# One net on one core: first norm, low-rank parts, scan products and log_dt loads rewritten

## The chip, the cores and the metric

The kernel runs on one core of a Trainium2 chip, as one program. The metric is the device time of a launch in microseconds, here the median of several runs. TensorE (PE in the profile) does the matrix products, VectorE (DVE) and ScalarE (ACT) the elementwise work, GpSimd (POOL) small powers and some memory moves, SyncE (SP) issues most of the transfers. All values are fp32. Each fp32 product appears as two PE instructions in the profile. The large weights are split into a high and a low part of 12 significant bits each, and a product then takes three instructions of a single pass ("mm3").

## The reference

The input is one sequence of 1024 tokens of 1024 features (D). Two layers and a hybrid block follow.

- Layer 0: RMS norm, a gated linear recurrence mixer ("hawk", width 1280), then a SwiGLU feed-forward part (width 2816) and a per-layer embedding: `h = h + (p[0] @ wp) * sigmoid(rms_norm(h) @ wg)`.
- Layer 1: RMS norm, an RWKV-7 time mix with 16 heads of 64, then the same feed-forward part and embedding with their own weights.
- A last RMS norm, then a block with a convolution of 31 taps and a complex diagonal state space of 32 groups with 64 states (S5), whose step sizes are `dt = exp(log_dt)`, one for each group.

The time mix is what most of the change touches. It shifts the tokens by one and makes six mixes of each token with the one before it; three go into r, k and v, three into low-rank parts:

```python
w = -softplus(-(w0 + tanh(xw @ w1) @ w2)) - 0.5      # w1: D x 64, w2: 64 x D
a = sigmoid(a0 + (xa @ a1) @ a2)                     # a1: D x 64, a2: 64 x D
g = sigmoid(xg @ g1) @ g2                            # g1: D x 160, g2: 160 x D
S_t = S_{t-1} * decay_t + (S_{t-1} a_t) b_t^T + v_t k_t^T      # for each head, 64 x 64
y_t = S_t r_t
out = (group_norm(y) + sum(r * k * r_k) * v) * g @ w_o
```

Here a_t is minus the normalized key of a head and b_t that key times `a`.

## The kernel before

Activations lie feature-major: 128 features on the partitions, tokens along the free axis, in two halves of 512 tokens. The first two layers run one after the other: hawk until about 500 us, the first feed-forward part until 1190, the embedding, then the time mix from about 1340 to 2395 ("scan stage"), the second feed-forward part to 3170, the second embedding, and the hybrid block to the end. The S5 parameters are prepared by `s5_prep`, whose steps are issued between those of the scan's end and of the second feed-forward part.

**First norm.** `load_rows` brings in 512 tokens as four tiles of 128 tokens x 1024 features; `turn_rows` transposes them on PE into feature-major tiles `h`. `square` then squares each of the eight tiles on ACT (L312) and adds them up on DVE (L313). `rstd_bcast` sums over the partitions on PE (L273), takes the power on GpSimd (L290), and spreads the factor over all partitions on PE (L281). L328 scales the tiles.

**Scan stage.** Its parts are Python generators that yield a step (engine, estimated us, what it waits for, a PSUM bank to take or give back) before the instructions of that step. `weave_` keeps a rough clock for each engine and always issues the step that would start first. So the order on every queue is written by estimates, and a changed estimate moves steps everywhere in the stage. PSUM banks by tag: two `mm`, three `g`, two `ch`, one `y`.

- `rwkv_dense` takes four segments of 256 tokens. A segment has 28 units: 24 of 128 columns for r, k and v (mm3, L249 to L251), and four for the first low-rank factors (L885, plain fp32). The two that belong to `w` and `a` (mixes 1 and 4) use the same 128 weight columns, 64 of `w1` beside 64 of `a1`; each computes all 128 and keeps half. Then `finish` runs for each of the eight head pairs of a segment. `lora2` multiplies the second low-rank factors (L926): 64 rows for w, 64 for a, 128 and 32 for g. Keys are normalized: per-head sums on PE (`heads_sum`, L1431), the reciprocal on DVE, and `heads_bcast` (L1438), which gives every feature of a head its token's value. Results go to DRAM.
- `rwkv_scan` takes 16 chunks of 64 tokens. `inner` (L1100) multiplies keys and queries in a chunk: for four head pairs at a time, first the four even heads (partitions 0 to 63) into one `g` bank, then the four odd heads (64 to 127) into another; DVE masks each bank (L1104). `diagonal`, `blocks`, `inverse`, `inverted` and `whole` invert a triangular matrix: its 32 x 32 blocks by substitution on DVE and GpSimd, with a way through DRAM (stores L1157, loads L1168, both on SP's queue), the rest by products L1179 and L1189. `chain` carries the state S (L1244 to L1274). `outs` makes y from the state (L1289, 64 x 64) and from the chunk itself (L1291, 128 x 64), and `post` does the group norm and the gate, again with `heads_bcast`.
- `rwkv_out` is the last projection.

**log_dt.** `s5_prep` first loads the S5 parameters on GpSimd's queue. The 32 values of log_dt go to all partitions (L1479). Then two further loads (L1481) bring the even groups' values to the lower and the odd ones' to the upper 64 partitions, every second value of the row.

Of the kernel before, what the change touches and what calls it, by code (L numbers as in the profile page):

```python
# [14 lines left out]
P = 128  # L15
# [41 lines left out]
class Net:  # L57
    """Feature-major activations: tile [128 features, 512 tokens] per (k, half)."""
# [16 lines left out]
    def open_group(self, T, W, S, L, psum):  # L75
        """Pools of one part of the net: T and S slots of [128, 516], weight slots, PSUM banks per tag."""
# [6 lines left out]
    def open_work(self, W, S, L, psum):  # L83
        """All of them but T anew."""
# [60 lines left out]
    def s(self, dt=F32, n=HT):  # L145
        """scratch [128, n <= 516]"""
# [3 lines left out]
    def extra(self, tag, shape, dt, every, bufs):  # L150
        """now and then a slot of the pool on the right, where that is for more of the others"""
# [7 lines left out]
    def ld(self, src=None, n=HT, rows=P):  # L159
        """tile for a load; loads have slots of their own, for they run ahead"""  # L160
# [66 lines left out]
    def load_ws(self, srcs, nk, m, tag="w"):  # L227
        """srcs: DRAM APs arranged [p, nk, n] for columns c..c+n; returns hi, lo tiles [P, nk, m]"""
# [17 lines left out]
    def mm3(self, ps, w, x, first, last):  # L246
        """ps += w.T @ x with w = (hi, lo), x = (hi, lo)"""
# [5 lines left out]
    # W columns [c0, c0+128) for all nk row tiles  # L253
# [3 lines left out]
    def lin(self, w, xs, nk):  # L257
        """xs: list of (hi, lo) per k -> PSUM tile"""
# [6 lines left out]
    def rstd_bcast(self, acc, scale, eps, acc2=None):  # L265
        """acc [128, 512] -> PSUM [128, 512]: (sum over partitions * scale + eps)^-0.5 on all partitions; with acc2,
        for which that is the factor of another norm: that one and the product of both"""
# [25 lines left out]
        rs = root(sums(acc))  # L293
# [8 lines left out]
    def square(self, h, k, half, gain=None):  # L302
        """h[k][half] is final: its part of the sum of squares (and of that of the products with the gain)"""
# [54 lines left out]

    def load_T(self, src, nk, sink):
# [1926 lines left out]
```

## Time and profile before

| what | us |
|---|---|
| median of 3 runs | 4188.85 |
| the runs | 4186.73, 4188.85, 4215.79 |
| the profiled execution, first to last instruction | 4186.6 |
| PE busy (22510 instructions) | 3949.4 (94%) |
| DVE busy | 2544.7 (61%) |
| ACT busy | 1466.1 (35%) |
| POOL busy | 179.3 (4%) |

The mean granted TensorE clock is 0.957 of full speed. The profile lists each engine's busy time, tables of windows in which the same busy times stand for a stretch with the clock and the share of the 16 DMA engines, groups of instructions by line and shape, and a timeline whose rows put together neighbouring instructions of one line. A busy time of PE includes the pipeline's drain, so the distance from one row's start to the next row's start is the better measure of what a group costs. "Idle before <- X" names what an engine waited for.

### The profile page before, as it was taken

The numbers are of one execution on the slowest core, as the hardware profiler recorded it, in microseconds if no ns is written. First come the engines' busy times: TensorE is split into PE (matmuls) and PEld (weight loads), VectorE is DVE, ScalarE is ACT, GpSimd is POOL, SyncE is SP. The second block draws the span as 40 slices with busy tenths as digits, with TensorE's granted clock in tenths as the row PEclk, the third lists the DMA queues.
The fourth block names the chain that finished last, engine by engine and source line by source line (L and its number), as shares of the span: only waits on it lengthen the run. The fifth ranks groups of instructions, "written<-read, shape, count | busy, mean of one in ns | idle before, by whom it ended". The sixth has DMA issues, their size and how long they took to land.

```text
span 4186.6 us, 58441 instructions
## 1 busy us (share of the span) xinstructions
PE 3949.4 (94%) x22510; PEld 3216.6 (77%) x22510; DVE 2544.7 (61%) x5192; ACT 1466.1 (35%) x2491; POOL 179.3 (4%) x376
## 2 busy tenths in 40 slices
PE   6998999999988999999999699999999999999899
PEld 5776788888877877777867587888887877888687
DVE  6665733333364678777756476354536599997655
ACT  4455511111132665554542241111113332222533
POOL 0000000000000000000000101010100000000000
PEclk8999999999998999989979799999999999999999
DMA  3111111111122789676776541212211244332775
GB/s 103 48 47 34 51 46 51 41 56 51 34 67 88 216 252 237 174 209 170 194 194 173 97 127 52 63 49 66 63 49 58 71 119 118 109 115 96 236 226 186
DMA packets 695830, 464.49 MB, mean 111 GB/s; under 512 B 197956, under 2 KB 620800, under 8 KB 695552
## 3 DMA queue, kind: packets, MB, share of 16 engines
q1 hardware_dynamic: 514272, 367.80, 30.0%
q10 hardware_dynamic: 175872, 83.90, 7.3%
q0 software_dynamic: 5408, 9.06, 1.1%
q8 instruction: 177, 2.90, 0.3%
q14 instruction: 101, 0.83, 0.1%
HBM read 355.51 MB, written 106.69 MB: 110 GB/s over the span
## 4 chain that ended last, share of the span: by engine, by line
PE 69%; DVE 12%; DMA 7%; ACT 5%; issue 4%; SPq 1%; POOL 1%; ACTq 0%; DVEq 0%; POOLq 0%
PE mm L249 15%; PE mm L251 14%; PE mm L250 14%; PE ob L249 4%; PE ob L250 4%; PE ob L251 4%; DVE cy L1882 3%; PE g L1100 2%; PE g L926 1%; PE g L1438 1%; PE y L1291 1%; DMA BK<-bkD 1%; PE y L1289 1%; DVE w L863 1%; PE mm L2073 1%
## 5 line engine op out<-in xcount | busy, mean ns | idle before, releaser
L249 PE MATMUL mm<-T,w 128*128 128x512 f32 (+1 forms) x2944 | 1152.6, 393 | 47.1 <-ACT w L215 22.5
L251 PE MATMUL mm<-T,w 128*128 128x512 f32 (+1 forms) x2944 | 1149.9, 391 | 9.6 <-DVE w L216 9.6
L250 PE MATMUL mm<-T,w 128*128 128x512 f32 (+1 forms) x2944 | 1150.3, 392 | 1.1 <-DVE T L1380 0.9
L249 PEld LDWEIGHTS mm<-T,w 128*128 128x128 f32 x2944 | 558.6, 190 | 174.3 <-ACT w L215 26.9
L251 PEld LDWEIGHTS mm<-T,w 128*128 128x128 f32 x2944 | 559.0, 190 | 126.8 <-DVE w L216 12.1
L250 PEld LDWEIGHTS mm<-T,w 128*128 128x128 f32 x2944 | 559.7, 190 | 117.5 <-DVE T L1380 1.7
L215 ACT CAST w<-wraw 128x1024 fp32r<-128x1024 f32 (+1 forms) x286 | 288.4, 1014 | 988.8 <-PE mm L250 700.2
L216 DVE TENSOR_TENSOR w<-wraw,w 128x1024 fp32r<-128x1024 f32 (+1 forms) x286 | 335.1, 1177 | 373.9 <-ACT w L215 371.1
L389 DVE TENSOR_TENSOR h<-ob,h 128x512 f32<-128x512 f32 x416 | 286.1, 690 | 230.7 <-PE ob L251 227.5
L249 PE MATMUL ob<-S,w 128*128 128x512 f32 x896 | 359.2, 401 | 21.7 <-DVE h L389 21.1
L1882 DVE SCALAR_TENSOR_TENSOR cy<-cu,pv,cy 128x512 f32<-128x512 f32 x480 | 350.9, 749 | 12.3 <-ACT cy L1880 2.6
L250 PE MATMUL ob<-S,w 128*128 128x512 f32 x896 | 354.7, 396 | 0.2 <-DVE S L216 0.2
L251 PE MATMUL ob<-S,w 128*128 128x512 f32 x896 | 354.7, 396 | 0.0
L249 PE MATMUL mm<-M,w 128*128 128x256 f32 x768 | 255.1, 332 | 16.4 <-ACT M L837 8.5
L250 PE MATMUL mm<-N,w 128*128 128x256 f32 x768 | 229.7, 299 | 4.4 <-DVE N L839 4.3
L251 PE MATMUL mm<-M,w 128*128 128x256 f32 x768 | 229.8, 299 | 4.3 <-DVE w L863 4.0
L249 PEld LDWEIGHTS ob<-S,w 128*128 128x128 f32 x896 | 169.9, 190 | 70.2 <-DVE h L389 30.2
L251 PEld LDWEIGHTS ob<-S,w 128*128 128x128 f32 x896 | 169.7, 189 | 38.6
L250 PEld LDWEIGHTS ob<-S,w 128*128 128x128 f32 x896 | 170.1, 190 | 36.3 <-DVE S L216 0.6
L249 PEld LDWEIGHTS mm<-M,w 128*128 128x128 f32 x768 | 157.0, 204 | 50.3 <-issue 23.3
L439 DVE TENSOR_TENSOR S<-mm,S 128x512 f32<-128x512 f32 x88 | 60.8, 690 | 211.7 <-PE mm L251 209.8
L215 ACT CAST S<-S 128x512 fp32r<-128x512 f32 x128 | 79.3, 620 | 266.3 <-DVE S L439 154.4
(458 smaller groups left out, 5431.9 us busy)
## 6 DMA issues: line engine op xcount, KB each, us to landing
wraw<-in_rw_w_rkv_dram ACTq DMA_DIRECT2D x96, 512.0 KB
wraw<-in_ffn_w_in_dram SPq DMA_DIRECT2D x88, 512.0 KB
wraw<-in_w_in_dram SPq DMA_DIRECT2D x48, 512.0 KB
wraw<-in_ffn_w_out_dram SPq DMA_DIRECT2D x44, 512.0 KB
BK<-bkD SPq DMA_DIRECT2D x64, 256.0 KB
wraw<-in_rw_w_o_dram ACTq DMA_DIRECT2D x24, 512.0 KB
wraw<-in_lru_w_in_dram SPq DMA_DIRECT2D x20, 512.0 KB
wraw<-in_ple_w_gate_dram SPq DMA_DIRECT2D x16, 512.0 KB
```

The source lines that it names most:

```text
L215: self.nc.scalar.copy(hi, x)
L216: self.nc.vector.tensor_sub(lo, x, hi.bitcast(F32))
L249: nc.tensor.matmul(ps, w[0], x[0], start=first, stop=False)
L250: nc.tensor.matmul(ps, w[0], x[1], start=False, stop=False)
L251: nc.tensor.matmul(ps, w[1], x[0], start=False, stop=last)
L389: nc.vector.tensor_add(h[m][half], ps, h[m][half])
L439: nc.vector.tensor_mul(a, ps, sg.pop((b, j, half)))
L863: nc.vector.tensor_sub(wl.rearrange(fl), r.rearrange(fl), wh.bitcast(F32).rearrange(fl))
L926: nc.tensor.matmul(ps, lw[r0:r1, slot, :], HW[hx][r0:r1], start=x == 0, stop=x == len(rows) - 1)
L1100: nc.tensor.matmul(g[:, 128 * x : 128 * x + 128], bk[rs, x].rearrange("p a b -> p (a b)"), qt[rs, j0 + x].rearrange("p a b -> p (a b)"), s ...
L1289: nc.tensor.matmul(o[rs], s[rs, x], qz[rs, j, 1, :], start=True, stop=False)
L1882: nc.vector.scalar_tensor_tensor(y, x[:, k : k + HT], cw(k), y, ALU.mult, ALU.add)
```

## The change

It has seven parts, and the planner's estimates of the changed steps are adjusted with them.

1. `square_rows`: the sums of squares of the first norm come from the token-major rows, by four ACT instructions of 128 x 1024 that sum along the features; `root` takes them as they are, and L273, L312 and L313 fall away there.
2. The second low-rank factors get four slots in DRAM instead of three, padded with zeros (six stores in `rwkv_consts`), and `lora2` always multiplies 128 rows. The tile `l` of a pair grows from 192 to 256 KB. The last sigmoid is taken on all 128 rows.
3. The units of mixes 1 and 4 become one, whose products go to 64 columns each, 27 units instead of 28 in a segment. The weights of this unit are loaded once instead of twice.
4. `heads_bcast` multiplies 128 x 128 once where it did 128 x 64 twice; ACT (in `post`) or DVE (in `finish`) first spreads the values over 64 columns.
5. `inner` takes two `g` banks together and alternates between the even and the odd head.
6. `outs` does all state products of a half chunk first and then all others.
7. The two loads of L1481 go; two DVE copies from the loaded values take their place.

Comments and docstrings are dropped too, and line numbers move. The diff, cut to its core:

```diff
-        rs = root(sums(acc))
+        rs = root(acc if acc.shape[-1] == 4 else sums(acc))
...
+    def square_rows(self, rows, half):
+
+        self.acc[half] = ss = self.tiny("ss", (P, 4), 2)
+        for c, r in enumerate(rows):
+            sq = self.wp.tile(list(r.shape), F32, tag="wh", name=self.n("sq"), bufs=self.nW[1])
+            self.nc.scalar.activation(sq, r, AF.Square, accum_out=ss[:, c : c + 1])
...
-        self.lwD = d((P, KD, 3, P), "lwD")
+
+        self.lwD = d((P, KD, 4, P), "lwD")
         I = self.I
-        for j, rows, src in ((0, slice(0, 64), I["rw_w2"][0]), (0, slice(64, P), I["rw_a2"][0]),
-                             (1, slice(0, P), I["rw_g2"][0][0:P]), (2, slice(0, 96), I["rw_g2"][0][0:96]), (2, slice(96, P), I["rw_g2"][0][P : P + 32])):
-            nc.sync.dma_start(self.lwD[rows, :, j], src.rearrange("p (j n) -> p j n", j=KD))
-        # per head pair the decays between chunk middles; at the segments' ends in two factors
+        zero = self.s()
+        nc.vector.memset(zero, 0.0)
+        for j, rows, src in ((0, slice(0, 64), I["rw_w2"][0]), (0, slice(64, P), None), (1, slice(0, 64), None),
+                             (1, slice(64, P), I["rw_a2"][0]), (2, slice(0, P), I["rw_g2"][0][0:P]),
+                             (3, slice(0, 96), None), (3, slice(96, P), I["rw_g2"][0][P : P + 32])):
+            if src is None:
+                for y in (0, 4):
+                    nc.sync.dma_start(self.lwD[rows, y : y + 4, j], zero[rows].rearrange("p (j n) -> p j n", j=4))
+            else:
+                nc.sync.dma_start(self.lwD[rows, :, j], src.rearrange("p (j n) -> p j n", j=KD))
...
-        low = [(1, both, (AF.Tanh, 0, 64, 0)), (4, both, (AF.Copy, 64, 128, 0)),
-               (5, w128(G1, 0), (AF.Sigmoid, 0, 128, 1)), (5, w128(G1, 32), (AF.Sigmoid, 96, 128, 2))]
+
+        low = [((1, 4), both, ((AF.Tanh, 0, 64, 0), (AF.Copy, 64, 128, 0))),
+               (5, w128(G1, 0), (AF.Sigmoid, 0, 128, 1)), (5, w128(G1, 32), (AF.Sigmoid, 0, 128, 2))]
...
-            if (u[0], 0) not in order:
+            if isinstance(u[0], tuple):
+                order += [(i, k + y) for k in range(0, KD, 2) for i in u[0] for y in range(2)]
+            elif (u[0], 0) not in order:
...
+                if isinstance(i, tuple):
+                    w = W.pop(x)
+                    for k in range(0, KD, 2):
+                        end = k == KD - 2
+                        sig = [("p", x)] * end + [("free", freed + y) for y in range(4)]
+                        wait = [("mix", seg, z, k + y) for z in i for y in range(2)] + [("w", x)] * (k == 0)
+                        ps = yield E("P", 1.74 * f, lat=0.15 if end else 0.0, wait=wait, sig=sig, bank=None if k else "mm")
+                        if k == 0:
+                            PSU[x] = ps
+                        freed += 4
+                        for y in range(2):
+                            for z, c in zip(i, rsl):
+                                nc.tensor.matmul(PSU[x][c, 0:n], w[:, k + y, c], M.pop((seg, z, k + y)),
+                                                 start=k + y == 0, stop=k + y == KD - 1)
+                    continue
...
         def lora2(ps, lw, rows):
             ps = ps[:, 0:n]
-            for x, (slot, hx, r0, r1) in enumerate(rows):
-                nc.tensor.matmul(ps, lw[r0:r1, slot, :], HW[hx][r0:r1], start=x == 0, stop=x == len(rows) - 1)
+            for x, (slot, hx) in enumerate(rows):
+                nc.tensor.matmul(ps, lw[:, slot, :], HW[hx], start=x == 0, stop=x == len(rows) - 1)
             return ps
...
-                raw = self.top.tile([P, 3, P], F32, tag=f"l2{x % nld}", name=self.n("l2"), bufs=1)
+                raw = self.top.tile([P, 4, P], F32, tag=f"l2{x % nld}", name=self.n("l2"), bufs=1)
...
-                    zw = lora2(pz, lw, [(0, 0, 0, 64)])
+                    zw = lora2(pz, lw, [(0, 0)])
...
-                    za = lora2(pz, lw, [(0, 0, 64, 128)])
+                    za = lora2(pz, lw, [(1, 0)])
...
-                    zo = lora2(pz, lw, [(1, 1, 0, P), (2, 2, 96, P)])
+                    zo = lora2(pz, lw, [(2, 1), (3, 2)])
...
-                    yield E("V", 0.2, rel=pz)
+                    yield E("V", 0.45, rel=pz)
                     rn = self.tiny(f"rn{q}", (P, 8), 2)[:, 0 : n // 64]
                     nc.vector.tensor_scalar(rn, st, 1e-24, None, ALU.max)
+                    rx = sq.rearrange("p (a b) -> p a b", b=64)
                     nc.vector.reciprocal(rn, rn)
-                    pz = yield E("P", 1.0 * f, bank="g", par=True, use=0.9)
-                    pb = self.heads_bcast(rn, pz, n // P)
+                    nc.vector.tensor_copy(rx, rn.unsqueeze(2).to_broadcast([P, n // 64, 64]))
+                    pz = yield E("P", 0.25, bank="g", par=True, use=0.9)
+                    pb = self.heads_bcast(rx, pz, n // P)
...
-                    for hd, rs in enumerate(rsl):
-                        x = 2 * c + j0 // 4
-                        g = yield E("P", 0.87, bank="g", use=0.5, wait=own(c) + past(c - NAM if c < NT else -1) + [("q", c), ("bk", x), "xn"],
-                                    sig=[("bf", x)] if hd else ())
-                        am, bk, qt = AM(c), BK[x], QT(c)
-                        for x in range(4):
+
+                    x = 2 * c + j0 // 4
+                    gs = [(yield E("P", 0.0, lat=0.0, bank="g", wait=own(c) + past(c - NAM if c < NT else -1) + [("q", c), ("bk", x), "xn"]))]
+                    gs.append((yield E("P", 1.0, bank="g", sig=[("bf", x)])))
+                    am, bk, qt = AM(c), BK[x], QT(c)
+                    for x in range(4):
+                        for g, rs in zip(gs, rsl):
                             nc.tensor.matmul(g[:, 128 * x : 128 * x + 128],
                                              bk[rs, x].rearrange("p a b -> p (a b)"),
                                              qt[rs, j0 + x].rearrange("p a b -> p (a b)"), start=True, stop=True)
+                    for hd, g in enumerate(gs):
...
-                y = yield E("P", 1.3 if c else 0.62, bank="y", use=0.6, wait=[("S", c, h)])
+                y = yield E("P", 1.2 if c else 0.62, bank="y", use=0.6, wait=[("S", c, h)])
                 s = st[h][c]
+
+                for x in range(4) if c else ():
+                    for rs in rsl:
+                        nc.tensor.matmul(y[rs, 64 * x : 64 * x + 64], s[rs, x], qz[rs, 4 * h + x, 1, :],
+                                         start=x == 0, stop=False, skip_group_check=True)
                 for x in range(4):
-                    j = 4 * h + x
-                    o = y[:, 64 * x : 64 * x + 64]
-                    if c:
-                        for hd, rs in enumerate(rsl):
-                            nc.tensor.matmul(o[rs], s[rs, x], qz[rs, j, 1, :], start=True, stop=False)
                     for hd, rs in enumerate(rsl):
-                        nc.tensor.matmul(o[rs], uv[:, j, hd, :], am[:, j, hd, 1, :], start=not c, stop=True)
+                        nc.tensor.matmul(y[rs, 64 * x : 64 * x + 64], uv[:, 4 * h + x, hd, :], am[:, 4 * h + x, hd, 1, :],
+                                         start=not c and x == 0, stop=x == 3, skip_group_check=True)
...
-                ps = yield E("P", 1.04, bank="g", use=0.9)
-                b = self.heads_bcast(rs, ps)
+                yield E("A", 0.48)
+                rx = self.tiny("psq", (P, HT), 1).rearrange("p (a b) -> p a b", b=64)
+                nc.scalar.copy(rx, rs.unsqueeze(2).to_broadcast([P, 8, 64]))
+                ps = yield E("P", 0.5, bank="g", use=0.9)
+                b = self.heads_bcast(rx, ps)
...
         for c in range(n):
-            for hd in range(2):
-                self.nc.tensor.matmul(bc[64 * hd : 64 * hd + 64, c * P : (c + 1) * P],
-                                      x[:, 2 * c + hd : 2 * c + hd + 1].to_broadcast([P, 64]), self.ident,
-                                      start=True, stop=True)
+            self.nc.tensor.matmul(bc[:, c * P : (c + 1) * P],
+                                  x[:, 2 * c : 2 * c + 2].rearrange("p a b -> p (a b)"), self.ident, start=True, stop=True)
...
-            for b in range(2):
-                dma(dt[64 * b : 64 * b + 64, 32:48], ldt[b:32:2].partition_broadcast(64))
...
+            yield V(16)
+            nc.vector.tensor_copy(dt[lo, 32:48], dt[lo, 0:32:2])
+            yield V(16)
+            nc.vector.tensor_copy(dt[hi, 32:48], dt[hi, 1:32:2])
...
+            net.square_rows(rows[0], 0)
...
+                net.square_rows(rows[1], 1)
...
-                  (net.reopen([("u", net.NSEG * 28 - 1)], ["rtop"], True), 0.0)]
+                  (net.reopen([("u", net.NSEG * 27 - 1)], ["rtop"], True), 0.0)]
```

On PE, in an early chunk of the scan, `y` is the tile of `outs`, `St` the state, `AM` the masked products, `UV` the chunk's values. Before:

```order
L1244 MATMUL ch_16741<-UV_8766,AM_11470 64x64 x2
L1247 MATMUL ch_16741<-St_16732,QT_8759 64x64 x2
L1289 MATMUL y_16766<-QT_8758,St_16098 64x64 x2
L1291 MATMUL y_16766<-AM_8786,UV_8765 64x64 x2
L1289 MATMUL y_16766<-QT_8758,St_16098 64x64 x2
L1291 MATMUL y_16766<-AM_8786,UV_8765 64x64 x2
...
L1100 MATMUL g_16789<-QT_8760,BK_16102 128x128 x4
```

And with the change, a half chunk of the same steps:

```order
L249 MATMUL mm_17421<-M_16655,w_17087 128x256
L250 MATMUL mm_17421<-N_16656,w_17087 128x256
L251 MATMUL mm_17421<-M_16655,w_17088 128x256
L1329 MATMUL y_17428<-QT_8728,St_17107 64x64 x8
L1333 MATMUL y_17428<-AM_11474,UV_8735 64x64 x8
L249 MATMUL mm_17421<-M_16672,w_17087 128x256
```

Eight groups of two products that alternate between lines have become two groups of eight.

On PE again, `inner` (L1100 before) between the weight products `mm` of the dense part; `g` are banks of that tag. Before:

```order
L885 MATMUL mm_16894<-M_16682,wraw_16477 128x256
L1100 MATMUL g_16941<-QT_8760,BK_16883 128x128 x4
L885 MATMUL mm_16894<-M_16690,wraw_16477 128x256
L1100 MATMUL g_16955<-QT_8760,BK_16883 128x128 x4
L1438 MATMUL g_16963<-ident,hr_16932 64x128 x8
L885 MATMUL mm_16894<-M_16703,wraw_16477 128x256
```

And with the change, where its line is L1141:

```order
L251 MATMUL mm_17090<-M_16793,w_17005 128x256
L1141 MATMUL g_17336<-QT_8727,BK_16582 128x128
L1141 MATMUL g_17340<-QT_8727,BK_16582 128x128
L1141 MATMUL g_17336<-QT_8727,BK_16582 128x128
L1141 MATMUL g_17340<-QT_8727,BK_16582 128x128
...
L1306 MATMUL ch_17118<-UV_8735,BT_8736 64x64 x8
```

Two steps of four products into one bank each, with other work between them, have become one step of eight that alternates between two banks.

On DVE at the program's start, where `L` is the sum of squares, `pv` the parameters' columns, `rs` the norm's factor and L328 scales the first tiles. Before:

```order
L313 TENSOR_TENSOR L_213<-L_213,S_233 128x512
L477 TENSOR_SCALAR sp_303<-sp_302 128x10
L289 TENSOR_SCALAR rs_241<-ms_236 128x4
L328 SCALAR_TENSOR_TENSOR S_250<-h_162,pv,ms_245 128x512
L328 SCALAR_TENSOR_TENSOR S_256<-h_169,pv,ms_245 128x512
```

And with the change:

```order
L289 TENSOR_SCALAR rs_222<-ss_157 128x4
L2176 COPY h_178<-mm_173 128x512
...
L484 TENSOR_SCALAR sp_284<-sp_283 128x10
L207 COPY pv<-ms_145 128x44
L328 SCALAR_TENSOR_TENSOR S_231<-h_171,pv,ms_226 128x512
```

The factor's first step has moved from behind the seven sums to the front of DVE's queue, and the last of the parameter copies now stands right ahead of the first scaling.

## Rows read from the trace of the kernel before

**Rows 1.** The page's chain that ended last, by engine.

```profile
PE 69%; DVE 12%; DMA 7%; ACT 5%; issue 4%; SPq 1%; POOL 1%; ACTq 0%; DVEq 0%; POOLq 0%
```

**Rows 2.** Windows: length; busy us of PE, PEld, DVE, ACT, POOL; clock; DMA share; GB/s.

```profile
1440.00:1700.00 260.00, 243.39 (x1619) 199.11 (x1618) 202.44 (x540) 167.71 (x379) 19.88 (x66) 0.95 0.89 238
1700.00:2165.00 465.00, 450.94 (x5230) 365.57 (x5229) 337.28 (x1110) 236.49 (x541) 35.81 (x84) 0.91 0.68 183
```

**Rows 3.** Timeline of SP and PE at the scan's end: start, us, engine, line, operation.

```profile
2282.16 2.52 SPq L1157 DMA_DIRECT2D yiD<-YB  x4
2286.18 1.81 SPq L1168 DMA_DIRECT2D YF<-yiD  x4
...
2340.65 21.20 SPq L1157 DMA_DIRECT2D yiD<-YB  x4
...
2364.91 1.81 SPq L1168 DMA_DIRECT2D YF<-yiD  x4
...
2367.25 0.31 PE L1179 MATMUL g<-XT,AM 32*32 32x32 f32 x2 [26.58 <-DVE XT L1173]
```

**Rows 4.** Timeline of the program's start.

```profile
20.47 7.30 SPq L236 DMA_DIRECT2D wraw<-in_lru_w_in_dram  x4
...
26.29 1.87 PE L273 MATMUL ms<-ones,L 128*128 128x1 f32 x8 [5.57 <-DVE L L313]
...
31.72 2.06 DVE L328 SCALAR_TENSOR_TENSOR S<-h,pv,ms 128x512 f32<-128x512 f32 x3 [3.35 <-PE ms L281]
```

**Rows 5.** Timeline of PE amid the scan.

```profile
1748.61 1.09 PE L1438 MATMUL g<-ident,hr 128*64 128x128 f32 x16
1749.63 0.33 PE L1289 MATMUL y<-QT,St 64*64 64x64 f32 x4
1749.89 0.34 PE L1291 MATMUL y<-AM,UV 128*64 128x64 f32 x4
...
1751.63 0.64 PE L1264 MATMUL ch<-UV,BT 128*64 128x64 f32 x16
1752.20 1.16 PE L1100 MATMUL g<-QT,BK 64*128 64x128 f32 x8
1753.29 0.38 PE L249 MATMUL mm<-M,w 128*128 128x256 f32 x1
```

**Rows 6.** Timeline of PE in `chain`, two groups of one shape.

```profile
1712.37 0.28 PE L1244 MATMUL ch<-UV,AM 64*64 64x64 f32 x4
1712.49 0.28 PE L1247 MATMUL ch<-St,QT 64*64 64x64 f32 x4
```

**Rows 7.** Timeline of PE around a low-rank product.

```profile
1454.61 0.70 PE L926 MATMUL g<-HW,l 64*128 64x256 f32 x2
1455.24 0.38 PE L249 MATMUL mm<-M,w 128*128 128x256 f32 x1
1455.46 0.28 PE L250 MATMUL mm<-N,w 128*128 128x256 f32 x1
1455.58 0.28 PE L251 MATMUL mm<-M,w 128*128 128x256 f32 x1
```

**Rows 8.** Groups by line and form: count, busy us, mean ns of one, idle before.

```profile
L885 PE MATMUL mm<-M,wraw 128*128 128x256 f32 x256 | 63.3, 391 | 0.4 <-DVE M L827 0.4
L1104 DVE TENSOR_TENSOR AM<-g,msk 128x512 f32<-128x512 f32 x64 | 44.0, 687 | 42.9 <-PE g L1100 42.9
L1219 ACT COPY BT<-g 128x512 f32<-128x512 f32 x32 | 18.7, 585 | 27.1 <-PE g L1216 27.0
L1015 DVE TENSOR_TENSOR BKs<-L,F 128x256 f32<-128x256 f32 x32 | 13.4, 420 | 0.5
```

**Rows 9.** A window, L926's instructions alone (columns: PE, PEld).

```profile
1440.00:1700.00 260.00, 43.30 (x128) 19.61 (x128) 0.95 0.89 238
```

**Rows 10.** Line L1481: its instructions, and the time to landing.

```profile
L1481 POOL DMA_DIRECT2D pv<-in_ssm_log_dt_dram x2: 817/836/855, 2338.2 to 2339.0; - x2
DMA to landing us min/median/max: 13.2/18.0/22.9
```

More of the change, by code (lines that the diff above doesn't have):

```diff
@@ L792, in rwkv_dense @@
         W, M, HW, PSU = {}, {}, {}, {}
+        rsl = [slice(0, 64), slice(64, P)]
         w128 = lambda w, c0: [(self.wcols(w, c0, KD), 0, P)]
         both = [(self.wcols(W1, 0, KD, 64), 0, 64), (self.wcols(A1, 0, KD, 64), 64, 64)]
-        low = [(1, both, (AF.Tanh, 0, 64, 0)), (4, both, (AF.Copy, 64, 128, 0)),
-               (5, w128(G1, 0), (AF.Sigmoid, 0, 128, 1)), (5, w128(G1, 32), (AF.Sigmoid, 96, 128, 2))]
+        low = [((1, 4), both, ((AF.Tanh, 0, 64, 0), (AF.Copy, 64, 128, 0))),
+               (5, w128(G1, 0), (AF.Sigmoid, 0, 128, 1)), (5, w128(G1, 32), (AF.Sigmoid, 0, 128, 2))]
         rkv = lambda i, mi: [(mi, w128(Wr[i], m * P), (i, m)) for m in range(KD)]
@@ L844, in weights @@
             ahead = 0
-            exact = lambda x: str(units[jobs[x][1]][0]) in EX[jobs[x][0]]
+            exact = lambda x: isinstance(units[jobs[x][1]][0], tuple) or str(units[jobs[x][1]][0]) in EX[jobs[x][0]]
             for x, (seg, u) in enumerate(jobs):
@@ L895, in evac @@
                 w = [("p", x)]
-                if len(what) == 2:
+                if isinstance(what[0], tuple):
+                    if seg:
+                        w += [("fin", seg - 1, j) for j in range(KD)]
+                    for func, r0, r1, slot in what:
+                        yield E("A", AE, wait=w, rel=(lambda: PSU[x]) if r1 == P else None, sig=[("u", x)] if r1 == P else [])
+                        if r0 == 0:
+                            HW[slot] = top(f"HW{slot}", (P, n), 1)
+                        nc.scalar.activation(HW[slot][r0:r1], PSU[x][r0:r1, 0:n], func)
+                    PSU.pop(x)
+                elif len(what) == 2:
                     i, m = what
@@ L948, in finish @@
                     x_ = seg * KD + j
-                    pz = yield E("P", 0.87 * f, wait=[("fl", x_)], bank="g", use=0.5)
+                    pz = yield E("P", 0.87 * f, wait=[("fl", x_)], bank="g")
                     lw, k, r, v = FL.pop(x_)
-                    zw = lora2(pz, lw, [(0, 0, 0, 64)])
+                    zw = lora2(pz, lw, [(0, 0)])
                     sg = fs(65 * nch)
@@ L956, in finish @@
                     nc.scalar.activation(c65(sg)[:, :, 1:], c65(sg)[:, :, 1:], AF.Copy, bias=0.5, scale=0.5)
-                    pz = yield E("P", 0.87 * f, bank="g", use=0.5)
-                    za = lora2(pz, lw, [(0, 0, 64, 128)])
+                    pz = yield E("P", 0.87 * f, bank="g")
+                    za = lora2(pz, lw, [(1, 0)])
                     yield E("A", AE, rel=pz, par=True)
@@ L967, in finish @@
                     nc.vector.tensor_sub(c65(csm), c65(cs), c65(cs)[:, :, 32:33].to_broadcast([P, nch, 65]))
-                    pz = yield E("P", 1.74 * f, bank="g", sig=[("fin", seg, j)], use=0.6)
-                    zo = lora2(pz, lw, [(1, 1, 0, P), (2, 2, 96, P)])
+                    pz = yield E("P", 1.74 * f, bank="g", sig=[("fin", seg, j)])
+                    zo = lora2(pz, lw, [(2, 1), (3, 2)])
                     yield E("A", AE, rel=pz, par=True)
@@ L1471, in main @@
         def main():
-            yield E("S", 9, 1.22, wait=list(wait))
+            yield E("S", 7, 1.22, wait=list(wait))
             rows = small()
```

14 lines of the change are left out of this document (5 added, 9 removed).

## The prediction

> **What bounds the kernel now.** I read the page's chain of waits first: TensorE (PE) holds 69% of it, VectorE (DVE) 12%, transfers 7% [rows 1]. Then the busy time by stretches of the scan stage [rows 2]. PE is busy 243 of 260 us in 1440 to 1700 and 451 of 465 us in 1700 to 2165, while DVE is at 78% and 73% and ScalarE (ACT) at 65% and 51%. So PE's own instructions set the pace there. One warning stands in the same rows: in 1440 to 1700 the DMA engines are busy 0.89 of the time, in 1700 to 2165 only 0.68. The scan's end is different: there PE stands idle for 26.58 us before one product [rows 3]. That is a wait, not work. The start is the third place: PE waits for the first norm, and that norm's first result comes at 31.72 us [rows 4].
>
> The sum is made against the profiled execution, 4186.6 us from first to last instruction; the fastest of the three runs took 4186.73 us, so next to nothing lies around the span, and the median of the runs, 4188.85 us, is 2 us above it.
>
> **The products that stop changing shape.** In the row of products [rows 5] eight groups of four alternate between 64x64 and 128x64; from 1749.63 to 1751.63 they take 2.00 us, 0.26 us a group, though a group holds only 0.12 us of products when its neighbour has the same shape [rows 6] (1712.37 to 1712.49). A change of shape so costs some 0.14 us. Sorted, a half chunk takes 4 x 0.12 for the state products and 0.57 for the 16 of 128x64 (L1264, the same shape and count, from 1751.63 to 1752.20 [rows 5]), about 1.07 us. `outs` saves 0.93 us on each of 30 half chunks: **28 us**.
>
> `inner` issues eight instructions (four heads) of 64 rows x 128 columns in 1.09 us [rows 5] (1752.20 to 1753.29), then later eight more for the other heads. Now the sixteen alternate between the two row halves. If the halves run side by side, a pair of groups costs about 1.1 instead of 2.2 us. No row of before has two tiles that differ in rows alone. The nearest are the 64x64 products [rows 6], which differ in rows and columns. An instruction of `inner` takes 0.11 us for 128 columns once the change of shape (0.2 us) is taken off its eight; one of 64 columns alone would take 0.055, and four of them 0.22, but four take 0.12. So about 1.8 run at once. Bounds for the 32 pairs: 0 (they queue) to 35 us. I take **35**, by that nearest row.
>
> The low-rank products go the other way, from part of the rows to all of them. Two instructions over 64 rows and 256 columns hold PE from 1454.61 to 1455.24, 0.63 us, and the wide product behind them takes 0.22 us until its successor starts, where the next takes 0.12 [rows 7]. Full rows of the same width (L885) cost 63.3 us for 256 instructions, some of them at the lower clock [rows 8]: at most 0.25, and 0.22 us where the clock is full, so two make 0.43. I put entering at about the price of leaving, 0.09 us. An excursion then costs 0.20 + 0.10 + 0.09 = 0.39 us more than staying. There are three in each of 32 head pairs (w, a, and the 32-row part of g): **37 us**. Bounds: half of that, where two excursions already lie side by side, and 37. The Trainium skill (TensorEngine Tiling (Array Packing), When to Use Tiling) speaks against this: a contraction of 64 or 32 rows is to be tiled, not filled up; by it this part would gain nothing. The fourth rival below carries that case.
>
> `heads_bcast` has half the instructions, each of 128 columns: for four tiles sixteen took 1.02 us [rows 5] (1748.61 to 1749.63), eight wide ones at 0.11 us take 0.87, and both ends no longer change shape (0.19, as above). That is 0.34 us on 16 chunks, and about as much on 32 pairs: **16 us**. Merging the two 64-column units takes a quarter of the L885 instructions' time if the column halves overlap as in [rows 5] L1264: 63.3/4 = 16, less imperfect overlap, **14 us** (bounds 4 and 16).
>
> What is added: a DVE copy of 128x256 in each pair (0.42 us [rows 8], 32 x 0.42 = 13 us on an engine at 73 to 78%), and an ACT copy of 128x512 in each chunk (0.585, 16 x 0.585 = 9 us on one at 51 to 65%). Both stretch chains that PE does not wait for while other work is ready; only the last chunk's ACT copy, 0.6 us, lies on the path. One 512 KB weight load fewer per segment and 64 KB more per pair in `l` give 0. The six zero fills on SP's queue and the memset fall in the first feed-forward, whose PE is busy all the time: 0. A rougher order of the planner is not priced; `order` keeps the same sequence of stages.
>
> The instructions sum to 28 + 35 + 37 + 16 + 14 = 130 us. Not all of it arrives. Half of the low-rank instructions (128 of 256) [rows 9] lie in 1440 to 1700; with the pairs, copies and merges there this is 37 us of the 130, but DMA at 0.89 leaves room for 260 x 0.11 = 29. I take 24. Before 1440 there is one merge, 3.5 us, in a stretch that waits for other things: 2. In 1700 to 2165 there are 70 us; DVE at 0.73 gets more to do in less time, so 42, six tenths. After 2165 there are 20 us: 13. Together **81 us**.
>
> **The strided loads.** In chunk 15, the last, SP starts to issue the four `yiD` stores at 2340.65 and is stuck on them for 21.2 us, so the loads behind them (L1168) begin at 2364.91, and PE stands idle for 26.58 us before L1179 [rows 3]. In chunk 14 the same two steps begin at 2282.16 and 2286.18: 4.0 us instead of 24.3. What falls into that time is L1481: its two loads of 4 KB, issued on POOL's queue just before, at 2338, land only after 13.2 and 22.9 us [rows 10]. They are the transfers that go; the copies that replace them read a contiguous load. Saved: 24.3 - 4.0 = **20 us**. Late next is DVE's transpose, then the last post step.
>
> **The start.** Before, the norm's sums wait for ACT squares and seven DVE adds; PE begins them at 26.29, and the first scaled tile is at 31.72 [rows 4]. The squares from rows need only four ACT steps of 128x1024, about 1.1 us each, twice the 128x512 copy of [rows 8], after the rows have landed. Then the parameters' columns are the gate, at some 22 us in the order of DVE. But the four first weight loads are only issued from 20.47 on, which takes 7.30 us [rows 4], so I take 6 of the 9 us for this half, and 2 for the second half's sums: **8 us** (bounds 3 and 12).
>
> Sum: 81 + 20 + 8 = 109; 4186.6 - 109 = **4078 us**.
>
> **The rivals.**
> 1. Transfers keep the pace of 1440 to 1700 and DVE that of the next stretch: 10 us arrive of 37, a third (23) of 70, 6 of 20, 2 before. With 28 for start and loads that is 69: 4118 us. For it: DMA at 0.89 and DVE at 78%; against it: PE's busy 94% in the same row. Chance 0.20.
> 2. Everything arrives, PE being the bound throughout: 130 + 28 = 158, 4029 us. For it: 97% PE in 1700 to 2165. Against it: the copies on DVE. Chance 0.12.
> 3. Row halves queue behind each other: 35 x 0.62 = 22 less, 4100 us. Chance 0.10.
> 4. Full rows cost as much as the part did: 37 x 0.62 = 23 less, 4101 us. Against it: the 0.63 us of [rows 7] beside 0.43. Chance 0.04.
> 5. Slower. `inner` now holds two of the three `g` banks until two mask products of 0.69 us [rows 8] have run behind one more DVE step of that size; the other steps that need a `g` bank queue on the third. At 2.1 us for each of 32 pairs this costs 66 us; PE, no longer dense, falls in 1700 to 2165 from a mean grant of 0.91 to 0.75 and its 451 us [rows 2] grow by 96. 4078 + 66 + 96 = 4240 us. It decides once the pauses and the clock together pass 109 us, 3.4 us a pair. Against it: PE idled only 14 us of 465 [rows 2], so DVE has kept up with these products. Chance 0.03.
> 6. The change does not reach the path at all but for the loads: 4165 us. Chance 0.03.
>
> My forecast has the remaining 0.48. The range reaches from 4034 (most of rival 2's side is left out) to 4132, which takes in rivals 1, 3 and 4 with the bounds of the start and of `inner`. What can be told from no change is 1%, 42 us. Faster than 4147: 0.90. Within 1%: 0.07. Slower than 4231: 0.03.
>
> **What would show it.** `outs` as two groups of eight, 1.1 us a half chunk; sixteen `inner` instructions in about 1.1 us; low-rank pairs at 0.43 us with no 0.1 us lost behind them; four `yiD` issues in about 2.5 us in chunk 15 and no idle PE before L1179's counterpart; the first scaled tile near 24 us. The prediction is wrong if PE idles more than some 60 us in 1340 to 2345, if the granted clock there falls below 0.85, or if DMA is at 1.0 while PE waits for weights.

## The result and the profile after

The changed kernel takes 4093.34 us (median of 4 runs, 4090.12 to 4097.04), 0.976 of the time before (95% interval 0.972 to 0.979), so about 95 us less by the medians; 4078 was forecast, 4034 to 4132 the range. Measured again with the experiments it gave 0.978 (0.976 to 0.981). The profiled execution has a span of 4095.0 us, 91.6 less than before.

Where the 91.6 us come from can be read by following the same instructions through both traces. The wide products (L249 in both) are issued 4904 times in either kernel. The first comes 5 us earlier, the 101st 18 us; until the scan stage (the 1600th, near 1240 us) the lead stays at 18. At the start of the second feed-forward part (the 2700th, near 2440) it is 90, and so it stays to the end. So **18 us come from the first 135 us of the program, 72 from the scan stage, and nothing from the rest.**

The chain of waits on the page has moved away from TensorE (69% before [rows 1]):

```profile
PE 62%; DVE 16%; DMA 8%; issue 7%; ACT 5%; POOL 1%; SPq 1%; ACTq 0%; DVEq 0%; POOLq 0%
```

The windows of the dense part, to be read beside [rows 2] (the columns are the same; the windows are moved by the lead):

```profile
1422.00:1660.00 238.00, 208.54 (x1486) 183.60 (x1485) 192.45 (x512) 157.34 (x358) 22.41 (x66) 0.94 0.90 251
1660.00:2112.00 452.00, 402.17 (x5180) 345.61 (x5180) 344.97 (x1171) 249.98 (x572) 38.24 (x85) 0.93 0.72 192
```

PE is busy 88% and 89% of the time where it was 94% and 97%. DVE has gone up to 81% and 76%, DMA hardly. The shapes of the products are as the change says. The PE timeline, `outs` and `inner`, beside [rows 5]:

```profile
1702.28 1.16 PE L1141 MATMUL g<-QT,BK 64*128 64x128 f32 x16
1703.37 0.33 PE L1286 MATMUL ch<-UV,AM 64*64 64x64 f32 x4
...
1979.95 0.68 PE L1329 MATMUL y<-QT,St 64*64 64x64 f32 x16
1980.56 0.69 PE L1333 MATMUL y<-AM,UV 128*64 128x64 f32 x16
1981.17 0.39 PE L249 MATMUL mm<-M,w 128*128 128x256 f32 x1
```

From start to start, a half chunk of `outs` takes 1.22 us instead of 2.0, and sixteen instructions of `inner` take 1.09 us, what eight took before. The spread in `finish` (L1483), and a low-rank product between wide ones, beside [rows 7]:

```profile
1444.02 0.71 PE L1483 MATMUL g<-ident,F 128*128 128x128 f32 x4
1444.49 0.37 PE L249 MATMUL mm<-M,w 128*128 128x256 f32 x1
...
1445.17 0.28 PE L251 MATMUL mm<-M,w 128*128 128x256 f32 x1
1445.29 0.59 PE L964 MATMUL g<-HW,l 128*128 128x256 f32 x2
1445.53 0.47 PE L249 MATMUL mm<-M,w 128*128 128x256 f32 x1
1445.83 0.28 PE L250 MATMUL mm<-N,w 128*128 128x256 f32 x1
```

The spread takes 0.47 us there. The low-rank pair and the wide product behind it take 0.54 us together, from 1445.29 to 1445.83; before they took 0.85. Groups by line over the whole trace (count, busy us, mean ns, idle before):

```profile
L964 PE MATMUL g<-HW,l 128*128 128x256 f32 x256 | 78.9, 413 | 6.8 <-DMA l<-lwD 3.0 <-ACT F L999 1.6 <-ACT F L1010 1.4
L1141 PE MATMUL g<-QT,BK 64*128 64x128 f32 x512 | 40.6, 300 | 6.4 <-DMA BK<-bkD 6.3
L918 PE MATMUL mm<-M,wraw 128*128 128x256 f32 x128 | 33.8, 405 | 3.6 <-DVE M L845 3.4
L1483 PE MATMUL g<-ident,F 128*128 128x128 f32 x128 | 23.2, 307 | 5.7 <-DVE TB L1188 2.5 <-DVE F L1032 2.0 <-DVE YB L1191 0.8
L900 PE MATMUL mm<-M,wraw 128*64 128x256 f32 x128 | 18.9, 391 | 0.8 <-DVE M L845 0.4
```

`inner` is busy 40.6 us; it was 80.0. L918 and L900 together are 52.7 where L885 was 63.3 [rows 8]. Adding up for each tile how long PE is held (up to the next start, idle time taken out), the stage needs 868 us of PE instead of 980: `inner` 37 less, low-rank products 29, `outs` 28, the merged unit 10, the spread 8. That is **112 us of the 130 forecast**. But 72 us is all the stage gave, with 20 of the strided loads in it, so some 52 of the 112 arrived (57, if only the 14.4 us by which PE's wait there grew shorter are put down to these loads). The rest is idle time of PE: 99 us before, 26.6 of it the wait for the strided loads; 143 now.

PE's longest waits in the scan stage of the changed kernel (line waited for: us in total, times, longest):

```profile
PE g L1221 <- DVE XT L1215: 12.2, 1, 12.2
PE g L1258 <- DMA BK<-bkD: 12.2, 5, 4.0
PE mm L250 <- DVE N L857: 12.2, 10, 4.2
PE mm L249 <- ACT M L855: 11.0, 8, 6.0
PE mm L249 <- ACT w L879: 7.6, 5, 2.6
PE g L1477 <- ACT psq L1349: 7.0, 2, 6.3
PE g L1141 <- DMA BK<-bkD: 6.3, 5, 2.8
```

No one of them is large. The mixes and weights (N, M, w), the loads of BK and the last post steps each keep PE a few us longer than before. Behind the 6.3 us for `psq` stands a store: ACT's square waits for `outD`, which is read from the same tile.

```profile
2121.12 0.60 ACT L1349 ACTIVATE psq<-g 128x512 f32<-128x512 f32 x1 [6.84 <-DMA outD<-psq]
```

In the last chunk, SP's stores and loads, to be read beside [rows 3]:

```profile
2272.43 2.52 SPq L1199 DMA_DIRECT2D yiD<-YB  x4
...
2276.72 1.81 SPq L1210 DMA_DIRECT2D YF<-yiD  x4
...
2282.15 1.43 PE L1221 MATMUL g<-XT,AM 32*32 32x32 f32 x32 [12.18 <-DVE XT L1215]
```

4.3 us between the two steps instead of 24.3, and PE's idle time falls from 26.58 to 12.18 us. At the program's start, beside [rows 4]:

```profile
22.69 2.06 DVE L328 SCALAR_TENSOR_TENSOR S<-h,pv,ms 128x512 f32<-128x512 f32 x3 [1.27 <-PE ms L281]
...
27.80 1.04 ACT L215 CAST w<-wraw 128x1024 fp32r<-128x1024 f32 x1 [1.14 <-DMA wraw<-in_lru_w_in_dram]
...
28.90 0.80 PE L249 MATMUL mm<-T,w 128*128 128x512 f32 x1 [6.25 <-ACT w L215]
```

The first scaled tile comes 9 us earlier, and then the first weights are late: ACT waits for their landing at 27.8.

### The profile page after: what moved, and what is told of

It is laid out like the page before. It is cut to its first block, busy times and chain, and to the rows that moved or that the text cites. A ratio compares the mean times of both kernels' runs of the same rounds, so it can differ in the third digit from the quotient of the medians.

```text
span 4095.0 us, 57944 instructions
## 1 busy us (share of the span) xinstructions
PE 3826.3 (93%) x22238; PEld 3151.6 (77%) x22238; DVE 2530.0 (62%) x5213; ACT 1472.3 (36%) x2507; POOL 184.2 (4%) x374
## 4 chain that ended last, share of the span: by engine, by line
PE 62%; DVE 16%; DMA 8%; issue 7%; ACT 5%; POOL 1%; SPq 1%; ACTq 0%; DVEq 0%; POOLq 0%
PE mm L249 14%; PE mm L251 14%; PE mm L250 13%; PE ob L249 4%; PE ob L250 4%; PE ob L251 4%; DVE cy L1928 4%; DMA wraw<-in_rw_w_rkv_dram 1%; DVE w L881 1%; PE mm L2119 1%; DVE w L216 1%; PE mm L2118 1%; PE mm L2117 1%; DMA GB<-abD 1%; DVE TB L1188 1%
## 5 line engine op out<-in xcount | busy, mean ns | idle before, releaser
L249 PE MATMUL mm<-T,w 128*128 128x512 f32 (+1 forms) x2944 | 1152.2, 393 | 49.6 <-ACT w L215 26.7
L251 PE MATMUL mm<-T,w 128*128 128x512 f32 (+1 forms) x2944 | 1148.0, 391 | 4.6 <-DVE w L216 4.6
L249 PEld LDWEIGHTS mm<-T,w 128*128 128x128 f32 x2944 | 558.3, 190 | 176.2 <-ACT w L215 31.0
L251 PEld LDWEIGHTS mm<-T,w 128*128 128x128 f32 x2944 | 558.5, 190 | 121.5 <-DVE w L216 6.4
L249 PE MATMUL ob<-S,w 128*128 128x512 f32 x896 | 360.3, 402 | 22.1 <-DVE h L396 21.2
L251 PE MATMUL ob<-S,w 128*128 128x512 f32 x896 | 355.6, 397 | 0.0
L249 PE MATMUL mm<-M,w 128*128 128x256 f32 x768 | 259.5, 338 | 18.9 <-ACT M L855 11.0
L251 PE MATMUL mm<-M,w 128*128 128x256 f32 x768 | 229.6, 299 | 5.7 <-DVE w L881 5.4
L249 PEld LDWEIGHTS ob<-S,w 128*128 128x128 f32 x896 | 170.3, 190 | 71.3 <-DVE h L396 30.6
L251 PEld LDWEIGHTS ob<-S,w 128*128 128x128 f32 x896 | 170.3, 190 | 39.0
L249 PEld LDWEIGHTS mm<-M,w 128*128 128x128 f32 x768 | 156.3, 204 | 32.2 <-ACT M L855 14.7
```

Source lines behind the costliest of these rows:

```text
L249: nc.tensor.matmul(ps, w[0], x[0], start=first, stop=False)
L251: nc.tensor.matmul(ps, w[1], x[0], start=False, stop=last)
```

## The experiments

My theory now: PE set the pace before; made 112 us shorter, it runs into the other engines' chains, and about half of what it is spared comes out as waits. The rival: PE still sets the pace, and the missing gain lies in single terms. The first kernels (names with b_) are the kernel before with one or two parts of the change, those with a_ the changed kernel with something altered. The merged unit was not tested apart. A ratio is against the kernel before as it ran beside: its median was 4201.2 us beside b_norm, b_loads, b_shapes and b_inner (10 runs, 4187.08 to 4215.27, so these differences in us run high), 4196.73 beside a_again, a_oldspread, a_partrows and a_oldouts, 4190.91 beside the rest. "Lead" is the gain by the same instructions of the two traces, as above.

**First norm from rows** (b_norm):

```diff
+            net.square_rows(rows[0], 0)
             net.turn_rows(rows[0], KD, 0, sink)
```

> The kernel before with the first norm's squares taken from the token-major rows, and nothing else. Theory A (the norm is all of the early gain; ACT and DVE, freed of eight squares and seven adds in each half, feed the first matrix products sooner): 18 us less, about 4170 us, and the 100th wide product 18 us earlier, of which the first one shows only 5. Theory B (only the earlier first tile counts, as predicted): 8 us less, about 4180 us.

4163.11 us, ratio 0.990 (0.987 to 0.994). The lead is 6 us at the first wide product and 22 at the 101st; before the scan stage it is 24. So theory A: the norm alone brings all of it. After its first products, PE waits less (timeline):

```profile
28.19 0.80 PE L249 MATMUL mm<-T,w 128*128 128x512 f32 x1 [6.12 <-ACT w L215]
...
32.27 0.51 PE L251 MATMUL mm<-T,w 128*128 128x512 f32 x1 [0.29 <-DVE w L216]
```

L251's first product came at 40.67 before, 8.4 us later; the second half's norm, which stopped PE three times near 60 us, gives the next 7, and the recurrence's first steps, which follow it on ACT and DVE, the rest.

**Strided loads** (b_loads):

```diff
-            for b in range(2):
-                dma(dt[64 * b : 64 * b + 64, 32:48], ldt[b:32:2].partition_broadcast(64))
+            yield V(16)
+            nc.vector.tensor_copy(dt[lo, 32:48], dt[lo, 0:32:2])
```

> The kernel before with the two strided log_dt loads replaced by two DVE copies, and nothing else; the order of the scan's instructions is that of before. Theory A (these loads hold up SP's stores in the last chunk): the four stores are issued in about 2.5 us instead of 21.2, PE's idle time of 26.6 us before the last chunk's first product falls to 5 to 7, and the run takes 20 us less, about 4168 us. Theory B (SP's queue is held up by its own traffic): the stall stays, 0 us.

4174.61 us, ratio 0.994 (0.992 to 0.997); the lead in the scan stage is 21 us. Theory A holds in place and size; PE's idle time there falls to 7.62 us:

```profile
2335.79 2.66 SPq L1157 DMA_DIRECT2D yiD<-YB  x4
2340.91 1.81 SPq L1168 DMA_DIRECT2D YF<-yiD  x4
...
2343.27 0.31 PE L1179 MATMUL g<-XT,AM 32*32 32x32 f32 x2 [7.62 <-DVE XT L1173]
```

**Outs and low-rank products in the old order of issue** (b_shapes), and **with the order written anew** (b_shapes2):

```diff
-            for x, (slot, hx, r0, r1) in enumerate(rows):
+            for x, (slot, hx) in enumerate(rows):
...
-                y = yield E("P", 1.3 if c else 0.62, bank="y", use=0.6, wait=[("S", c, h)])
+                y = yield E("P", 1.2 if c else 0.62, bank="y", use=0.6, wait=[("S", c, h)])
```

(`outs` is sorted as in the diff of the change; the second pair of lines only in b_shapes2.)

> The kernel before with outs sorted by shape and the second low-rank products over all rows, and the planner's estimates left as they were, so that steps are issued in the order of before. PE is spared about 28 + 29 us. Theory A (TensorE's instructions set the pace of the stage): 45 to 57 us less, 4131 to 4143 us. Theory B (vector work and transfers take over as soon as TensorE is faster): 15 to 30 us less, 4158 to 4173 us, and PE's idle time in the stage grows by the difference.

> The kernel before with outs sorted and the low-rank products over all rows, as measured once with the planner's old estimates (27 us of 54 us of TensorE time came back by the trace), now with the changed kernel's estimates for these steps, so that the order is written anew. Theory A (the old order was what kept half of the gain): 40 to 50 us less than before. Theory B (vector work and transfers take half of it in any order): 25 to 32 us less.

b_shapes: 4153.02 us, ratio 0.988 (0.985 to 0.992). b_shapes2: 4166.17 us, 0.993 (0.991 to 0.996). The two groups of products hold PE 54 and 57 us less; the lead in the stage is 30 and 21 us. The 30 come from the slowest of b_shapes' four executions (4164.69) and so run low. A new order by the planner gains nothing over the old one, so the order is not what keeps the other half. For b_shapes alone the ratio would allow theory A; its trace and b_shapes2 speak for B.

**Inner in turn** (b_inner):

```diff
+                    for x in range(4):
+                        for g, rs in zip(gs, rsl):
                             nc.tensor.matmul(g[:, 128 * x : 128 * x + 128],
```

> The kernel before with inner on two banks at a time, even and odd heads in turn, and the planner's estimate for it; nothing else. Both theories: sixteen instructions in about 1.15 us instead of 2.2, so 33 to 37 us less PE time. Theory A (TensorE sets the pace): 25 to 35 us less, 4153 to 4163 us. Theory B (vector work and transfers take over): 5 to 20 us less. Theory C (two of three banks held by inner hold up the other steps): nothing gained, or slower.

4153.99 us, ratio 0.988 (0.985 to 0.992), lead in the stage 42 us for 38 us of PE time: the whole, and a little of the clock with it. Theory A here; C falls, the two banks held at once cost nothing that shows. Sixteen instructions take what eight took, so the two row halves do run side by side:

```profile
1751.42 1.16 PE L1100 MATMUL g<-QT,BK 64*128 64x128 f32 x16
1752.51 0.38 PE L249 MATMUL mm<-M,w 128*128 128x256 f32 x1
```

The next ones start from the changed kernel. Beside it (a_again):

> The changed kernel as it is, as the reference for the three that follow: 0.976 of the time of before, about 4093 us.

4106.84 us, ratio 0.978 (0.976 to 0.981); its lead in the scan stage is 71.5 us, that of the first profile 71.8.

**The spread as before** (a_oldspread):

```diff
-                    nc.vector.tensor_copy(rx, rn.unsqueeze(2).to_broadcast([P, n // 64, 64]))
-                    pz = yield E("P", 0.25, bank="g", par=True, use=0.9)
+                    pz = yield E("P", 1.0 * f, bank="g", par=True, use=0.9)
```

> The changed kernel with heads_bcast as before (eight products of 128x64, no copies ahead of them, the planner's old estimates for it). TensorE gets about 8 us more to do, DVE 13 us less, ACT 9 us less. Theory A (after the change vector work and transfers set the pace of the dense part): equal or up to 15 us faster than the changed kernel. Theory B (TensorE still sets it): 5 to 10 us slower.

4098.27 us, ratio 0.976 (0.973 to 0.978), 8.6 us below a_again by the medians, lead in the stage 79. The intervals overlap; but the part of the change that spares PE 8 us gains nothing, and likely loses.

**Low-rank products over part of the rows again** (a_partrows):

```diff
-                nc.tensor.matmul(ps, lw[:, slot, :], HW[hx], ...
+                nc.tensor.matmul(ps, lw[r0:r1, slot, :], HW[hx][r0:r1], ...
```

> The changed kernel with the second low-rank products over 64, 64, 128 and 32 rows again, every instruction in the same place of every queue. TensorE gets 29 us more to do. Theory A (TensorE no longer sets the pace): 5 to 15 us slower than the changed kernel, about half of it or less. Theory B (it does): 25 to 30 us slower.

4145.61 us, ratio 0.987 (0.984 to 0.989): 39 us slower than a_again, more than either theory had. The windows of a_again and of this kernel over the same stretch:

```profile
1660.00:2110.00 450.00, 400.33 (x5208) 343.29 (x5207) 344.32 (x1165) 248.79 (x569) 38.18 (x84) 0.94 0.73 195
```

```profile
1660.00:2110.00 450.00, 415.03 (x4804) 339.50 (x4805) 327.87 (x1129) 238.65 (x540) 33.87 (x77) 0.86 0.69 186
```

With every instruction in the same place, the granted clock of these 450 us is 0.86 instead of 0.94 (a mixture of the levels 2.4 and 1.2 GHz). Over the whole stage the low-rank products hold PE for 95 us instead of 55, all other products for 21 us more, and PE waits 14 us less: 47 us by the trace, 39 by the medians. The change of the products alone was worth 29 us between the kernels before and after; the rest goes with the lower clock. That part rows as such lower the clock is not shown. In 1700 to 2165 the kernel before had 0.91 with them [rows 2], b_shapes 0.92 without them, and b_loads 0.94 with them. First b_shapes, then b_loads:

```profile
1700.00:2165.00 465.00, 428.43 (x5420) 363.90 (x5421) 351.18 (x1145) 245.96 (x562) 38.24 (x88) 0.92 0.76 203
```

```profile
1700.00:2165.00 465.00, 446.29 (x5297) 359.47 (x5296) 336.27 (x1106) 237.62 (x540) 34.98 (x84) 0.94 0.72 191
```

The Trainium skill's advice to row-tile a contraction of 64 or 32 rows (TensorEngine Tiling (Array Packing), When to Use Tiling) would have kept the old form. Where such products stand singly between wide ones, the measurement speaks against it. The Trainium skill also says (TensorEngine Tiling (Array Packing), Tiling Modes, Key Properties) that different tiles can load weights and multiply in parallel. `inner` agrees: sixteen instructions in 1.09 us, where eight of one row half took as long.

**Outs alternating again** (a_oldouts):

```diff
-                for x in range(4) if c else ():
-                    for rs in rsl:
...
+                    if c:
+                        for hd, rs in enumerate(rsl):
```

> The changed kernel with the products of outs alternating between the two shapes again, in the same places of the queues. TensorE gets 28 us more to do, about 20 of it in the dense part and 8 behind it, where the chain of the last chunks runs through outs. Theory A (TensorE no longer sets the pace of the dense part): 8 to 16 us slower than the changed kernel. Theory B (it does): 25 to 28 us slower.

4123.4 us, ratio 0.982 (0.980 to 0.984): 16.6 us slower than a_again; by the trace 21 us of the stage for 25 us of PE time. Between the theories, nearer to B by the trace and on A's edge by the medians.

**More vector work** (a_copy2) and **more transfers** (a_load2):

```diff
                     nc.vector.tensor_copy(rx, rn.unsqueeze(2).to_broadcast([P, n // 64, 64]))
+                    nc.vector.tensor_copy(rx, rn.unsqueeze(2).to_broadcast([P, n // 64, 64]))
```

```diff
                 nc.sync.dma_start(raw, self.lwD[:, j])
+                nc.sync.dma_start(self.dram.tile([P, 4, P], F32, name=self.n("dum")), self.lwD[:, j])
```

> The changed kernel with each of finish's 32 copies of 128x256 on DVE done twice, every instruction else in its place. DVE gets 32 x 0.42 = 13.5 us more to do. Theory A (DVE is what TensorE now waits for in the dense part): 8 to 14 us slower than the changed kernel. Theory B (DVE has slack): 0 to 4 us.

> The changed kernel with 32 more copies of 256 KB from DRAM to DRAM beside the pairs' loads, which nothing waits for; every instruction else in its place. That is 8 MB read and 8 MB written on top of about 200 MB in the scan stage. Theory A (the transfers are at their limit in the dense part): 20 to 35 us slower than the changed kernel. Theory B (they have slack, or only their latency counts): 0 to 8 us.

a_copy2: 4102.65 us, 0.978 (0.976 to 0.981). a_load2: 4110.47 us, 0.980 (0.977 to 0.982). Beside a_again's 0.978 neither is a difference. In the stage's lead they lose 10 and 7 us, in executions that were above (4113) and near (4109) their medians, against one of a_again that was below its own (4102). Up to 10 us can hide in either. That is not the 20 to 35 that transfers at their limit would have cost, so their throughput is no limit in itself. For DVE it stays open: 10 of 13.5 us would be theory A, and the medians say theory B.

**Old spread and two slots for BK** (a_best):

```diff
-NBK = 1
+NBK = 2
```

> The changed kernel with heads_bcast as before, which alone made it 8.6 us faster, and with two slots instead of one for the tile BK, whose loads TensorE waits for in 15 us of the changed kernel's scan (two small tiles get fewer slots to make room). Theory A (the wait for BK is on the path): 10 to 25 us faster than the changed kernel, 4070 to 4085 us. Theory B (BK's waits are cover for others): the 8.6 us alone.

4085.56 us, ratio 0.974 (0.971 to 0.976), the fastest version here, by the ratios 10 to 20 us below the changed kernel (0.976 and 0.978) and 8 below a_oldspread, from which it is not clearly separated. Its profiled execution, the fastest of the five (4069), has a lead of 99 us in the stage. So the time would allow theory A, but its mechanism isn't seen: PE waits for BK as long as in the changed kernel,

```profile
PE g L1256 <- DMA BK<-bkD: 15.6, 7, 5.7
PE g L1139 <- DMA BK<-bkD: 3.7, 2, 3.3
```

19 us in all, 18.5 in the changed kernel.

## Why the prediction came out as it did

- *The direction, and the size within the range*: right, 4093 for 4078. Some of it is luck, for two errors cancelled in part: the start was priced 10 us too low, the stage's instructions 29 too high.
- *The start, 8 us (bounds 3 and 12)*: too small. It brought 18 us there and 22 to 24 alone. I priced the first tile (9 us, late weights taken off; the first product indeed came only 5 earlier) but gave the second half's norm 2 us, from PE's own waits. In b_norm the lead is 6 us at the first product, 9 before the second half's norm, 15 behind it and 22 at the 101st product. The squares and sums also stood in ACT's and DVE's queues, ahead of the work for PE's next products. That the rest comes from there is read from the order of these queues; no run tests it apart.
- *The strided loads, 20 us*: right in cause, place and size (4.3 us between the steps for 24.3; 21 us alone). In the whole change PE's wait there shrank by 14.4 us only, because 12.18 us for DVE's transpose are left.
- *PE's instructions, 130 us*: 112. `inner` (37 for 35) and `outs` (28 for 28) are as priced, and the 64x64 row was the right neighbour for the row halves: rival 3 falls. The low-rank products are 29 for 37, though the price of a single excursion was right: at full clock, from the start of the wide product ahead of it to the end of the second one behind it, this takes 1.18 us with part rows and 0.79 with full rows (medians of 20 places before and 22 after), 0.39 less. But only a third of the 96 (33) lay between wide products without a wait; the others had a small product or a wait beside them, so the reason is likely, not shown. The merge is 10 for 14: a 64-column product holds PE for 0.14 us, more than half of the 0.24 of a full one. The spread is 8 for 16: in `finish`, where it has two tiles and not the four of the row that I priced, it saved 0.12 us a pair instead of 0.34.
- *The share that arrives, 81 us of 130*: this step failed; 52 arrived. I took six tenths in 1700 to 2165 by the room on DVE, and 24 of the 29 us that DMA left in 1440 to 1700. The runs show no such limit of the transfers (8 MB more each way cost at most 7 us), and leave it open for DVE (13.5 us more of copies cost between nothing and 10). What took the gain are PE's waits, spread over many steps: outside the wait for the strided loads they rose from some 73 to 131 us. By itself a part gave all (`inner`) or about half by the traces (the two shapes). Undone in the changed kernel, PE's time still counted for most of itself: 21 us of the stage for 25 of PE (`outs`), 47 for 62 (low-rank, the other products at the lower clock included). That is more than the half of my theory and speaks for its rival, that PE still sets much of the pace. So half is what this whole change gave, and not a rate at which the stage answers.
- *The signs of being wrong*: one of them came. I had named 60 us of idle PE in 1340 to 2345. The same stretch of the changed kernel, 1322 to 2255, has 115 us (second line). The sign was also badly set, as the kernel before already had 64 (first line). The clock (0.92) stayed above 0.85, and DMA (0.90 in the busiest window above) below 1.0.

```profile
1340.00:2345.00 1005.00, 941.31 (x9046) 773.34 (x9046) 704.75 (x2099) 515.58 (x1135) 72.14 (x173) 0.91 0.73 197
```

```profile
1322.00:2255.00 933.00, 817.93 (x8676) 702.25 (x8676) 684.67 (x2085) 515.16 (x1142) 70.65 (x163) 0.92 0.77 211
```

- *Copies that other work hides, priced at nothing*: doubtful. Without them and with the old spread the kernel was not slower, by the medians 8.6 us faster.
- *Rival 1* (transfers and DVE as the pace, 4118) had 41 us for the instructions where 52 came, nearer than the forecast's 81, but not the cause. *Rival 2* (everything arrives) falls with the 52. *Rivals 4, 5 and 6* fall: full rows are the largest single loss when undone, the two banks cost nothing that shows, and the stage gave 52 us more than the loads.

What remains open is which chain between the engines sets the stage's length now. The parts interact through the planner's order, and with PE at 89%, the page's chain in 1660 to 2112 is 168 us of PE (366 before, in 1680 to 2165), 103 of transfers' time, and 86 of DVE. In a_again, the same kernel, it is 226 of PE, 99 and 75, so these shares are rough. No run here isolates one of its links.

## What to carry to other kernels

When work is taken off the engine that sets the pace, price the shares part by part, but expect that a stage full of short dependent steps gives some of it back as waits. Here it was about half for the whole change, and the room on the other engines did not show it. A step moved off the start of a program can be worth more than the wait that it ends there: the norm's first result came 9 us earlier, the 101st product 22. And products of different shape should be grouped: here a change of shape cost 0.14 us, and a group of four small products 0.12.

## What the runs showed of the hardware

- With products over all 128 rows instead of 64 or 32, in the same places, the granted clock in 450 us of mixed work was 0.94 instead of 0.86 (a_again, a_partrows). On the kernel before no such difference shows: 0.91 with part rows, 0.92 with full rows (b_shapes).
- Two fp32 instructions over 64 rows and 256 columns, between products over all 128 rows, cost 0.39 us more than the same two padded with zeros to 128 rows (1.18 and 0.79 us with their neighbours).
- Two 64-row products of 128 columns in different PSUM banks run side by side: sixteen instructions in 1.09 us, eight of one half before in the same 1.09.
- Two small loads of every second 4-byte value, spread over 64 partitions, kept the store issues of another queue back: 21.2 us for four, 2.5 to 2.7 without them.
